# Placing the small products of a recurrent stage in TensorE's queue: one place and one bank for each kind, the turn of A ahead of the inverse, another last stage and opening

## The chip, the cores and the metric

The kernel runs on one core of a Trainium2 chip. The engines work side by side, each through its own queue in order: TensorE (PE, with its weight loads as PEld), VectorE (DVE), ScalarE (ACT), GpSimd (POOL) and SyncE (SP), which only issues transfers. The metric is the device time of one execution in microseconds (us). The kernel before took 3183.36 us, the median of three runs (3176.78, 3183.36 and 3184.9).

## The reference

One block of a streaming encoder, in float32: 2048 rows of width 1024.

```python
h = rms_norm(x, pre_mix_g);  proj = h @ w_in          # 1536 attention, 1792 RWKV, 2048 gate columns
y_a = chunk_band_attention(q, k, v, rel_bias)          # own chunk of 64 and 8 chunks before it
y_b = rwkv7_time_mix(p_rwkv, ...)                      # 8 heads of 64; delta rule over time:
#   state = state * w_t + (state @ a_t) b_t^T + v_t k_t^T;   y_t = state @ r_t
merged = sigmoid(gA) * (y_a @ proj_a) + sigmoid(gB) * (y_b @ proj_b)
x = x + rms_norm(merged @ w_out, post_mix_g)
x = x + rms_norm(relu(rms_norm(x, pre_ffn_g) @ w_up) ** 2 @ w_down, post_ffn_g)
```

## The kernel before

**Stages.** The 2048 rows are worked in four groups of 512 (g = 0 to 3). Each group goes through a recurrent stage (`phase_rwkv`), an attention stage and a merge; then two halves of 1024 rows each go through an up stage (`phase_up`) and a down stage (`phase_down`), which ends with the last norm and the output (`final`). The opening (`first_norm`) makes the first group's normed input.

**Dense products.** A projection of 128 columns (`dense`) is 24 TensorE matmuls of 128x512: weight and input are each split into a high and a low part, and three products of parts over 8 blocks of the inner dimension are summed in a bank of the pool `pd` (`psd` in the trace). A recurrent stage has 30 of them: 14 mixes (block 12 is the decay and rate input, 13 the gate input, p, 4 + p and 8 + p are r, k and v of head pair p) and 16 gates, so 720 dense matmuls. They are counted in the order of the program in the list `self.dl`; "place n" below means behind dense matmul n of the stage.

**Small products.** For each of the four head pairs p there are further: `lora` (tiles `ps_z`, `ps_a`), the sums of squares (`ps_ss`), the centred values (`ps_v`), the bonus (`ps_bonus`), the transposes of B and K (`ps_bk`), the chunk products (`ps_A`; 8 chunks in two halves, a matmul for each of the two heads, whose sums go to one bank a head), the turn of A (`ps_at`) and the products of values (`ps_w`). VectorE then inverts a 64x64 triangle for all chunks of two pairs at once (`rwkv_inverse`, 31 steps of two small operations each); `rwkv_blocks` joins the 32x32 blocks (`ps_t`), `rwkv_trans` makes the transition of each chunk (`ps_ug`, `ps_tq`, `ps_y`, `ps_s`), `recurrence` goes through the 8 chunks (for each chunk two matmuls into `ps_st` and two into `ps_y` for each head pair, then a VectorE step that makes the next state), and `rwkv_post` norms and gates the result (`ps_yt`, `ps_g`).

**Order.** A planner in the framework orders each engine's queue: it takes what is ready by its own model, the earlier in the program first. `queue_behind` ties an instruction behind another in the queue without a semaphore, and `place` does that with a place n among the stage's dense matmuls. Before, seven constants hold places: the blocks (`BLOCKS`), one turn (`TURNED`), one step of the recurrence (`FIFTH`), two parts of the bonus, the first chunk product (`SCORES`) and one pair's `ps_yt` (`TURNS`). `GATES` and `STEPS` say how many gates or steps of the recurrence are written between the parts of `rwkv_pre`. In the program, pairs 0 and 1 come first, then their inverse with gates, then the recurrence of pairs 0 and 1 woven into the preparation of pairs 2 and 3, then the second inverse and recurrence.

**Banks.** PSUM's 8 banks are two each for the pools `pd` (dense), `pa` (tag "a"), `pr` (tag "wus") and `py` (tag "y"). Nearly all small products go through the two banks of `pa`; the second half of the chunk products of pairs 0 and 1, the steps and `ps_yt` use `pr`; the outputs Y and `ps_g` use `py`.

**The end.** In the last step of `phase_down` each of four row tiles gets its last bank added (`gather`, L1469), and `final` squares it with a sum on ScalarE (L1480), multiplies by the gain on VectorE (L1481), adds two sums and takes the root on POOL (L1483, L143, L145), scales and adds x in two halves on VectorE (L1487) and stores (L1491).

Of the kernel before, what the change touches and what calls it, by code (L numbers as in the profile page):

```python
# [18 lines left out]
P = 128  # L19
D = 1024  # L20
# [14 lines left out]
STEPS = (1, 2, 1, 1, 1, 1, 1, 1, 1, 1, 1, 0, 0, 2, 1)  # L35
BLOCKS = ((412, 424), (640, 653))
TURNED = 438
FIFTH = 494
BONUS = {(0, 1): 138, (1, 0): 258}
SCORES = 150  # L40
TURNS = {1: (588, 592)}
# [15 lines left out]
class Block:  # L57
# [45 lines left out]

    def placed(self):

        for ins, n in self.places:
            self.queue_behind(ins, self.dl[n])
# [10 lines left out]
    def dense(self, col):  # L118
# [9 lines left out]
        if first:  # L128
# [5 lines left out]
            self.queue_behind(self.mm[0], self.last_transpose)  # L134
# [162 lines left out]
    def first_norm(self, sp, pt):  # L297
# [12 lines left out]
        squares = [self.root_of(sp, x, t) for t, x in enumerate(xs)]  # L310
# [113 lines left out]
    def lora(self, par, p):  # L424
        ps = self.pa.tile([P, G], F32, tag="a", name=("ps_z", "ps_a")[par])
        pc = slice(p * P, (p + 1) * P)
        self.nc.tensor.matmul(ps, self.wh[par][:, pc], self.lo[par], start=True, stop=False)
        self.nc.tensor.matmul(ps, self.wl[par][:, pc], self.lo[par], start=False, stop=True)
        return ps
# [14 lines left out]
    def rwkv_pre(self, g, p, rp, NA, between=lambda: None):  # L444
# [5 lines left out]
        self.mix(g, p, r)  # L450


        ps = self.lora(0, p)
        tw = self.tmp("tw")
        nc.scalar.activation(tw, ps, AF.Tanh, scale=0.5, bias=self.hw0[:, col])
        k = self.tmp("k")
        self.mix(g, 4 + p, k)

        ps = self.lora(1, p)
        ta = self.tmp("ta")  # L460
        nc.scalar.activation(ta, ps, AF.Tanh, scale=0.5, bias=self.ha0[:, col])
        v = self.tmp("v")
        self.mix(g, 8 + p, v)

# [7 lines left out]
        nc.scalar.activation(E[:, :, 1 : C + 1], cum3, AF.Exp)  # L472
# [11 lines left out]
        pss = self.pa.tile([P, GT, 2], F32, tag="a", name="ps_ss")  # L484
        for t in range(GT):
            nc.tensor.matmul(pss[:, t], sq[:, t * P : (t + 1) * P], self.bones2, start=True, stop=True)
# [33 lines left out]
        nc.vector.scalar_tensor_tensor(r, r, self.rk[:, col], tk, op0=ALU.mult, op1=ALU.mult)  # L520
        rh, rl = (self.tp.tile([P, G], F32R, tag="t", name="r" + x) for x in "hl")
        self.split(rh, rl, r)

        between()

        SV = rp.tile([P, NC, 2, C], F32, tag="SV", name="SV")
        psv = self.pa.tile([P, GT, P], F32, tag="a", name="ps_v")
        for t in range(GT):
            nc.tensor.matmul(psv[:, t], v[:, t * P : (t + 1) * P], self.cmat, start=True, stop=True)
        SVv = SV.rearrange("p (t h) e c -> p h t e c", h=2)  # L530
        for h in range(2):
            src = psv[h * C : h * C + C]
            nc.scalar.copy(SVv[C:P, h, :, 0], src[:, :, 0:C])
            self.values = nc.scalar.copy(SVv[0:C, h, :, 1], src[:, :, C:P]).ins
        R["SV"] = SV

        between()

        psb = self.pa.tile([P, G], F32, tag="a", name="ps_bonus")
        for i, x in enumerate((rh, rl)):  # L540
            mm = nc.tensor.matmul(psb, self.bones, x, start=i == 0, stop=i == 1)
            if (p, i) in BONUS:
                self.place(mm, BONUS[p, i])
# [4 lines left out]
        for h in range(2):  # L548
            cs = slice(h * 4, h * 4 + 4)
            pst = self.pa.tile([P, 4, 2, C], F32, tag="a", name="ps_bk")  # L550
            for j in range(4):
                nc.tensor.transpose(
                    pst[:, j].rearrange("p e f -> p (e f)"),
                    BK[:, h * 4 + j].rearrange("p s t -> p (s t)"), self.ident,
                )
            nc.vector.tensor_tensor(
                BR[:, cs, :, 0], pst, n2[:, cs, :, None].to_broadcast((P, 4, 2, C)), ALU.mult
            )

        between()  # L560
# [3 lines left out]
        for h in range(2):  # L564
            pool, tag = (self.pr, "wus") if p < 2 and h else (self.pa, "a")
            both = [pool.tile([P, 4, P], F32, tag=tag, name="ps_A") for _ in range(2)]
            for j in range(4):
                c = h * 4 + j
                for par, psA in enumerate(both):
# [5 lines left out]
                    if p == c == par == 0:  # L575
                        self.place(mm, SCORES)
            for par, psA in enumerate(both):
# [6 lines left out]
                for i in range(2):  # L584
                    hw = slice(par * C + 32 * i, par * C + 32 * i + 32)
                    cs = slice(h * 4, h * 4 + 4)
                    nc.scalar.copy(NA[hw, q, cs], BR[hw, cs, par, 2, 32 * i : 32 * i + 32])
        R["AR"], R["BR"] = AR, BR
        return R

    def rwkv_inverse(self, NA, rp):
# [23 lines left out]
        XD = ip.tile([P, 2, NC, 32], F32, tag="N", name="XD")  # L615
        nc.vector.transpose(XD, X1)
        XT = rp.tile([P, 2, NC, C], F32, tag="XT", bufs=1, name="XT")
        for par in range(2):
            r0 = par * C
            nc.gpsimd.memset(XT[r0 + 32 : r0 + 64, :, :, 0:32], 0.0)  # L620
            nc.scalar.copy(XT[r0 + 32 : r0 + 64, :, :, 32:64], XD[r0 + 32 : r0 + 64])
        for par in range(2):
            nc.gpsimd.tensor_copy(XT[par * C : par * C + 32, :, :, 0:32], XD[par * C : par * C + 32])
        self.X1, self.XT = X1, XT

    def rwkv_blocks(self, Rs, b):
# [3 lines left out]
        Z = self.ip.tile([P, 2, NC, 32], F32, tag="Z", name="Z")  # L630
# [16 lines left out]
        for mm, n in zip((first[0], second[0]), BLOCKS[b]):  # L647
            self.place(mm, n)
# [5 lines left out]
    def rwkv_trans(self, p, R):  # L654

        nc, xp = self.nc, self.xp
        AR, SV, XT, BR = (R[x] for x in ("AR", "SV", "XT", "BR"))
        rows = [slice(0, C), slice(C, P)]
        halves = [slice(0, 4), slice(4, 8)]

        WA = xp.tile([P, NC, 2, C], F32, tag="WA", bufs=1, name="WA")
        ps = self.pa.tile([P, 4, P], F32, tag="a", name="ps_at")
        for j in range(4):
            mm = nc.tensor.transpose(ps[:, j], AR[:, 1, 2 * j : 2 * j + 2].rearrange("p c t -> p (c t)"), self.ident)
            if p == j == 0:
                self.place(mm, TURNED)
# [3 lines left out]
        ps = self.pa.tile([P, NC, C], F32, tag="a", name="ps_w")  # L670
# [964 lines left out]
```

## Time and profile before

The profiled execution took 3181.86 us, of which its span, from the first to the last instruction, is 3180.2 us.

| stretch, us from the span's start | what | length, us | PE busy, us | DVE busy, us | ACT busy, us |
|---|---|---|---|---|---|
| 24 to 285 | recurrent stage, g = 0 | 261.0 | 258.70 | 184.99 | 130.92 |
| 478 to 748.6 | recurrent stage, g = 1 | 270.6 | 268.54 | 188.83 | 135.38 |
| 965 to 1236 | recurrent stage, g = 2 | 271.0 | 268.93 | 189.01 | 135.55 |
| 1453 to 1724 | recurrent stage, g = 3 | 271.0 | 268.93 | 189.25 | 135.68 |
| 1941 to 2246 | up stage, first half | 305.0 | 305.00 | 225.74 | 155.47 |
| 2555 to 2864 | up stage, second half | 309.0 | 306.65 | 230.99 | 155.92 |
| 2864 to 3169.2 | down stage, second half | 305.2 | 305.16 | 165.63 | 123.54 |
| 3169.2 to 3180.2 | after the last matmul | 11.0 | 0.00 | 6.14 | 1.34 |

A float32 matmul of the program (all small products but `ps_z`, `ps_a`, `ps_bonus` and `ps_g`) stands in the trace as two instructions: 64 chunk products of a stage are 128 rows of `ps_A`. A busy PE is not a PE at its peak: a matmul's busy time holds its latency, and neighbours overlap. Where the time of a matmul matters, the distance from one start to the next is to be read, from the starts in the timeline.

### The profile page before, as it was taken

To read this page: it belongs to the slowest core of one execution; us is meant where nothing else is said; L and a number is where in the kernel's file an instruction comes from. 1 tells how busy PE (TensorE), PEld (TensorE's weight loads), DVE (VectorE), ACT (ScalarE), POOL (GpSimd) and SP (SyncE) were. 2 spreads that over 40 slices of the span, in tenths; PEclk is the share of its full clock that TensorE was granted. 3 is DMA by queue.
4 is the path that set the end of the run, shared out by engine and by line. 5 is a ranking of instruction groups with operands and counts; after the bars stand their busy time and mean duration, and the time that the engine had idled before them with its cause. 6 is when DMAs were issued, how large, how long until landed. Compare 5 with 4: busy or idle time off the path is not lost.

```text
span 3180.2 us, 49723 instructions
## 1 busy us (share of the span) xinstructions
PE 3135.3 (99%) x18736; PEld 2567.8 (81%) x18736; DVE 2190.1 (69%) x3652; ACT 1617.5 (51%) x2639; POOL 570.8 (18%) x1087
## 2 busy tenths in 40 slices
PE   8999999999999999999999999999999999999998
PEld 6877788788888878888877888888888878888887
DVE  6776666777867676766776776877656668765564
ACT  5545645545745455745545745445543454444343
POOL 3121012122112122111122100221211122210000
PEclk9999999999999999999999999999999999999999
DMA  6245473257573256574246466554877766547664
GB/s 195 84 150 179 141 251 130 65 169 262 172 262 120 77 163 242 173 262 138 84 134 234 160 222 249 201 172 162 304 245 269 280 217 207 172 152 248 192 219 175
DMA packets 197477, 598.81 MB, mean 188 GB/s; under 512 B 25570, under 2 KB 25708, under 8 KB 197236
## 3 DMA queue, kind: packets, MB, share of 16 engines
q1 hardware_dynamic: 139124, 415.24, 40.0%
q0 software_dynamic: 48896, 163.61, 13.7%
q10 hardware_dynamic: 9216, 16.78, 1.4%
q8 instruction: 147, 2.41, 0.3%
q14 instruction: 94, 0.77, 0.1%
HBM read 431.67 MB, written 167.01 MB: 188 GB/s over the span
## 4 chain that ended last, share of the span: by engine, by line
PE 60%; issue 10%; POOL 2%; DMA 2%; ACT 2%; DVE 1%; SPq 0%; POOLq 0%; DVEq 0%; ACTq 0%
PE ps_dn L1454 19%; PE psd L92 16%; PE ps_u L92 9%; PE ps_o L1163 3%; PE ps_p L92 2%; PE ps_pv L1003 2%; POOL xd L1324 2%; PE ps_s L973 1%; PE ps_pt L992 1%; PE ps_A L571 1%; PE ps_tq L695 0%; DMA x<-in_x_dram 0%; PE ps_ht L1202 0%; PE ps_ug L684 0%; PE ps_st L723 0%
## 5 line engine op out<-in xcount | busy, mean ns | idle before, releaser
L1454 PE MATMUL ps_dn<-fop 128*128 128x512 f32 x2688 | 611.0, 389 | 0.5 <-DVE fop L83 0.5
L1454 PEld LDWEIGHTS ps_dn<-fop 128*128 128x128 f32 x2688 | 504.1, 188 | 105.4 <-DVE fop L83 0.9
L83 DVE TENSOR_TENSOR wlo<-wraw,whi 128x1024 fp32r<-128x1024 f32 x230 | 280.8, 1221 | 142.5 <-ACT whi L81 62.3
L81 ACT CAST whi<-wraw 128x1024 fp32r<-128x1024 f32 x232 | 243.4, 1049 | 232.5 <-PE psd L92 152.5
L92 PE MATMUL psd<-hh,whi 128*128 128x512 f32 x1328 | 355.7, 398 | 3.4 <-ACT k L400 3.4
L92 PE MATMUL psd<-hh,wlo 128*128 128x512 f32 x1328 | 358.1, 398 | 0.0
L92 PE MATMUL psd<-hl,whi 128*128 128x512 f32 x1328 | 356.3, 397 | 0.0
L92 PEld LDWEIGHTS psd<-hh,wlo 128*128 128x128 f32 x1328 | 243.6, 188 | 50.1
L92 PEld LDWEIGHTS psd<-hh,whi 128*128 128x128 f32 x1328 | 242.2, 188 | 51.7 <-ACT k L400 3.9
L92 PEld LDWEIGHTS psd<-hl,whi 128*128 128x128 f32 x1328 | 243.9, 188 | 47.3
L83 DVE TENSOR_TENSOR fop<-xraw,fop 128x1024 fp32r<-128x1024 f32 x112 | 137.0, 1223 | 175.3 <-ACT fop L81 174.9
L81 ACT CAST fop<-xraw 128x1024 fp32r<-128x1024 f32 x112 | 117.7, 1051 | 249.4 <-PE ps_dn L1454 189.6
L1324 POOL DMA_DIRECT2D xd<-X x192 | 103.7, 540 | 380.7 <-ACT X L1321 318.4
L83 DVE TENSOR_TENSOR fop<-wdraw,fop 128x1024 fp32r<-128x1024 f32 x112 | 136.6, 1220 | 19.0 <-ACT fop L81 18.8
L81 ACT CAST fop<-wdraw 128x1024 fp32r<-128x1024 f32 x112 | 117.7, 1051 | 36.7 <-DMA wdraw<-in_w_down_dram 21.7
L979 DVE CUSTOM_DVE_ANT_0 sc<-bias,ps_s 128x640 f32<-128x640 f32 (+4 forms) x128 | 93.8, 733 | 39.6 <-PE ps_s L973 23.5
L986 ACT ACTIVATE sc<-sc,mn 128x640 f32<-128x640 f32 (+4 forms) x128 | 97.8, 764 | 32.1 <-DVE mn L979 30.9
L997 DVE TENSOR_TENSOR PTl<-ps_pt,PTh 128x640 fp32r<-128x640 f32 (+4 forms) x128 | 94.4, 737 | 27.7 <-ACT PTh L996 26.8
L81 ACT CAST s12h<-s 128x1024 fp32r<-128x1024 f32 x32 | 33.7, 1053 | 155.2 <-PE ps_u L92 155.2
L92 PE MATMUL ps_p<-yh,whi 128*128 128x512 f32 x256 | 101.4, 399 | 2.7 <-ACT yh L81 1.7
L92 PE MATMUL ps_p<-yl,whi 128*128 128x512 f32 x256 | 101.2, 396 | 0.3 <-DVE yl L83 0.2
L1163 PE MATMUL ps_o<-whi,mh 128*128 128x512 f32 x256 | 100.4, 392 | 0.8 <-DVE o L1174 0.8
(370 smaller groups left out, 6731.8 us busy)
## 6 DMA issues: line engine op xcount, KB each, us to landing
wraw<-in_w_in_dram SPq DMA_DIRECT2D x168, 512.0 KB, 3.6
xraw<-xd SPq DMA_DIRECT2D x112, 512.0 KB, 4.3
xd<-X POOLq DMA_DIRECT2D x192, 256.0 KB, 4.6
wraw<-in_w_up_dram SPq DMA_DIRECT2D x80, 512.0 KB, 4.5
wdraw<-wd SPq DMA_DIRECT2D x64, 512.0 KB, 4.7
wdraw<-in_w_down_dram SPq DMA_DIRECT2D x48, 512.0 KB, 4.8
gd<-gate ACTq DMA_DIRECT2D x64, 256.0 KB, 2.2
wd<-cmb POOLq DMA_DIRECT2D x64, 256.0 KB, 4.0
```

Of the source, the lines that this page charges most:

```text
L81: high = self.high = self.nc.scalar.copy(hi, src)
L83: self.low = lower.tensor_tensor(lo, src, hi.bitcast(F32), ALU.subtract).ins
L92: mm.append(nc.tensor.matmul(ps, l, r, start=n == 0, stop=n == last).ins)
L571: mm = nc.tensor.matmul(psA[:, j].rearrange("p (s t) -> p s t", t=C), BK[rw, c].rearrange("p s t -> p (s t)"), AR[rw, :, c], start=True, s ...
L973: nc.tensor.matmul(pss[:, c0 + lo_ : c0 + lo_ + w], q[:, par, qs], Kv[:, k0 + lo_ : k0 + lo_ + w], start=i == 0, stop=i == 1,)
L979: least = nc.vector.tensor_tensor_reduce(sc[:, 0:n], bias[:, s0:640], pss[:, c0 : c0 + n], 1.0, 3.0e38, ALU.add, ALU.min, mn,)
L986: nc.scalar.activation(sc[:, 0:n], sc[:, 0:n], AF.Exp, scale=-1.0, bias=mn, accum_out=sm[:, col : col + 1])
L997: nc.vector.tensor_tensor(lv, pst[:, 0:nk], hv.bitcast(F32), ALU.subtract)
L1003: nc.tensor.matmul(pv[:, half], st, x[:, kt], start=i == 0, stop=i == len(terms) - 1)
L1163: nc.tensor.matmul(ps[t], l[:, k, ts], r[:, k % 2], start=k == 0 and j == 0, stop=k == KB - 1 and j == 2)
L1324: nc.gpsimd.dma_start(self.xd[q][i // 2][:, i % 2], src)
L1454: nc.tensor.matmul(ps, o[:, l, k, sl], o[:, r, k], start=start and n == 0, stop=stop and n == end)
```

## The change

1. The seven constants of places become one table `PINS`, with a place for the first matmul of each kind and pair, and `BANKS`, which gives some kinds a bank of `pr` ("r") or `py` ("y") in place of `pa` ("a").
2. The turn of A (`rwkv_turn`) and the products of values (`rwkv_values`) leave `rwkv_trans`; they are written ahead of the inverse or beside it. `rwkv_trans` then takes both pairs: first both `ps_ug`, then `ps_tq`, `ps_y` and `ps_s` of each. WA and GT get two buffers, S0 shares GT's.
3. The copies to NA are four a pair in place of eight. Z lies in XD's tile.
4. The order of the program: pairs 2 and 3 are prepared before the first recurrence is woven in (`STEPS`), pair 3's lora and values come later, `lora_g` (mix 13 and the load and split of g2) moves from the first inverse to behind the first recurrence, and the end of `rwkv_post` of pairs 2 and 3 is written ahead of the last gates.
5. The opening issues 38 matmuls of a constant (`bones`) around the four transposes, and 5 more between the first dense matmuls.
6. `final` of one tile is written behind the gather of the next; the root takes two POOL operations in place of three; in the second half the first columns' gain goes to a tile of its own, x has four buffers, and for the last four tiles the output is stored in two halves.

```diff
+STEPS = (0, 0, 0, 0, 0, 0, 0, 0, 0, 0, 0, 0, 0, 0, 5, 2)
+IDLE = (24, 0, 4, 4, 6)
+BETWEEN = 5
+LAST = 0
+PINS = {
+    "E3": 456, "na2": 462, "st05": 497, "g1": 602, "g3": 712, "g2": 702, "g0": 520,
+    "yt01": 520, "yt00": 520, "yt31": 712, "yt30": 712, "yt21": 700, "yt20": 700, "rh3": 472,
+    "x1": 626, "bk31": 474, "bk30": 474, "bo3": 474, "x0": 440,
+    "z0": 48, "a0": 48, "ss0": 110, "v0": 110, "bk00": 131, "bk01": 131, "bo0": 131, "at0": 131, "A00": 146, "A01": 146,
+    "z1": 146, "a1": 146, "ss1": 227, "v1": 227, "w0": 227, "bk10": 240, "bk11": 240, "bo1": 246, "at1": 240,
+    "A10": 258, "A11": 258, "z2": 290, "a2": 290, "w1": 290,
+    "ss2": 350, "v2": 350, "bk20": 384, "bk21": 384, "bo2": 390, "at2": 545, "A20": 396, "A21": 396,
+    "z3": 404, "a3": 404, "w2": 545, "t10": 440, "ss3": 456, "v3": 474, "t20": 456, "ug0": 470, "ug1": 470,
+    "at3": 600, "w3": 600, "yt10": 600, "yt11": 600, "t11": 626, "t21": 639, "ug2": 652, "ug3": 652,
+}
+BANKS = {
+    **{f"bk{p}{h}": "r" for p in range(2) for h in range(2)}, "A01": "r", "A11": "r",
+    "at0": "y", "z1": "y", "a1": "y", "w0": "y", "at1": "y", "w1": "y",
+    "bk20": "r", "bk21": "r", "at2": "a", "w2": "a", "A21": "r", "at3": "a", "w3": "a", "bo1": "y", "bo2": "y", "z3": "y", "a3": "y",
+}
...
+    def pin(self, mm, name):
+        if name in PINS:
+            self.place(mm, PINS[name])
+    def bank_of(self, name):
+        pool, tag = {"a": (self.pa, "a"), "r": (self.pr, "wus"), "y": (self.py, "y")}[BANKS.get(name, "a")]
+        return lambda shape, label: pool.tile(shape, F32, tag=tag, name=label)
...
-            self.queue_behind(self.mm[0], self.last_transpose)
+            self.queue_behind(self.mm[0], self.last_idle)
+            if self.idle is not None:
+                for i in range(BETWEEN):
+                    self.queue_behind(self.mm[i + 1], self.idle(1, self.mm[i]))
+                self.idle = None
...
+                mm = self.nc.tensor.matmul(
+                    idle, self.bones, self.bones[:, None, :].to_broadcast((P, 4, P)), start=True, stop=True
+                ).ins
...
+        turn(IDLE[0])
+        for t, x in enumerate(xs):
+            squares.append(self.root_of(sp, x, t))
+            self.queue_behind(self.last_transpose, last)
+            turn(IDLE[t + 1], self.last_transpose)
...
-            pool, tag = (self.pr, "wus") if p < 2 and h else (self.pa, "a")
-            both = [pool.tile([P, 4, P], F32, tag=tag, name="ps_A") for _ in range(2)]
+            bank = self.bank_of(f"A{p}{h}")
+            both = [bank([P, 4, P], "ps_A") for _ in range(2)]
...
+        for q, R in enumerate(Rs):
+            GT = R["GT"] = xp.tile([P, NC, C], F32, tag="GT", name="GT")
+            pool, tag = banks[q]
...
+            yield
+        for q, R in enumerate(Rs):
+            TQ = R["TQ"] = xp.tile([P, NC, 2, C], F32, tag="TQ", name="TQ")
...
-                    nc.scalar.activation(sq, u[t][:, ns], AF.Square, accum_out=ssq[:, n : n + 1])
-                    nc.vector.tensor_tensor(u[t][:, ns], u[t][:, ns], gt[:, ns], ALU.mult)
+                    nc.scalar.activation(sq, u[t][:, ns], AF.Square, scale=D ** -0.5, accum_out=ssq[:, n : n + 1])
+                    w = u[t][:, ns] if n or not half else op.tile([P, G], F32, tag="ug", name="ug")
+                    self.gained = nc.vector.tensor_tensor(w, u[t][:, ns], gt[:, ns], ALU.mult).ins
...
+                    if th == 0 and t + 1 < GT:
+                        self.queue_behind(scaled.ins, self.gained)
+                    if half and th == 0:
+                        nc.sync.dma_start(self.out[rows, ns], u[t][:, ns])
...
-                            advance(ends[t])
+                            advance(ends[t], 1)
+                            if t:
+                                advance(ends[t - 1])
```

More of the change, by code (lines that the diff above doesn't have):

```diff
@@ L309, in first_norm, with turn @@
         self.bank(pt)
-        squares = [self.root_of(sp, x, t) for t, x in enumerate(xs)]
+        idle = pt.tile([P, 4, P], F32, tag="tr", name="ps_idle")
+        last = None
+        def turn(n, behind=None):
+            nonlocal last
+            for i in range(n):
+                mm = self.nc.tensor.matmul(
+                    idle, self.bones, self.bones[:, None, :].to_broadcast((P, 4, P)), start=True, stop=True
+                ).ins
+                if behind is not None:
+                    self.queue_behind(mm, behind)
+                if last is not None:
+                    self.queue_behind(mm, last)
+                last = mm
+            return last
+        turn(IDLE[0])
+        squares = []
+        for t, x in enumerate(xs):
+            squares.append(self.root_of(sp, x, t))
+            self.queue_behind(self.last_transpose, last)
+            turn(IDLE[t + 1], self.last_transpose)
+        self.idle, self.last_idle = turn, last
         highs = self.scale_up(range(KB))
@@ L442, in lora_g, with rwkv_pre @@
         self.split(*self.lg, lg)
-    def rwkv_pre(self, g, p, rp, NA, between=lambda: None):
+    def rwkv_pre(self, g, p, rp, NA, out, between):
         nc = self.nc
@@ L646, in rwkv_blocks @@
                     second.append(mm)
-        for mm, n in zip((first[0], second[0]), BLOCKS[b]):
-            self.place(mm, n)
+        self.pin(first[0], f"t1{b}")
+        self.pin(second[0], f"t2{b}")
         for lo, hi in parts:
@@ L688, in rwkv_trans @@
-        yield
-        TQ = xp.tile([P, NC, 2, C], F32, tag="TQ", name="TQ")
-        for h, cs in enumerate(halves):
-            ps = self.pa.tile([P, 4, 2, C], F32, tag="a", name="ps_tq")
-            for j in range(4):
-                c = h * 4 + j
-                for par in range(2):
-                    nc.tensor.matmul(
-                        ps[rows[par], j], GT[rows[par], c], BR[rows[par], c, par, 0:2], start=True, stop=True
-                    )
-            nc.vector.tensor_tensor(
-                TQ[:, cs, 0], ps[:, :, 0], self.id64[:, None, :].to_broadcast((P, 4, C)), ALU.add
-            )
-            nc.vector.tensor_tensor(TQ[:, cs, 1], ps[:, :, 1], AR[:, 0, cs], ALU.add)
@@ L818, in rec_of @@
                 yield
-                for q in range(2):
-                    yield from self.rwkv_trans(2 * b + q, Rs[q])
-                    yield
+                yield from self.rwkv_trans(b, Rs)
                 yield from self.recurrence(b, Rs)
@@ L827, in phase_rwkv @@
             between = places(GATES, gate)
-            Rs = [self.rwkv_pre(g, q, rp, NA, between) for q in range(2)]
+            Rs, nxt = [], []
+            for q in range(2):
+                advance(self.rwkv_pre(g, q, rp, NA, Rs, between))
             advance(spread)
@@ L842, in phase_rwkv @@
             between = places(STEPS, lambda n: advance(rec, n))
-            nxt = [self.rwkv_pre(g, 2 + q, rp, NA, between) for q in range(2)]
-            inv = self.rwkv_inverse(NA, rp)
-            for n in (1, 4):
-                advance(rec, n)
-                gate()
+            second, third = (self.rwkv_pre(g, 2 + q, rp, NA, nxt, between) for q in range(2))
+            advance(second, 2)
+            advance(third, 1)
+            advance(second)
+            advance(third)
+            inv = self.rwkv_inverse(NA, rp, 1)
+            advance(rec, 1)
+            gate()
+            advance(rec, 4)
+            gate()
             advance(rec)
+            self.lora_g(g)
             post = [self.rwkv_post(q, Rs[q]) for q in range(2)]
@@ L851, in phase_rwkv @@
                 advance(p, 1)
+            for q in range(2):
+                nxt[q]["WA"] = self.rwkv_turn(2 + q, nxt[q]["AR"])
+                self.rwkv_values(2 + q, nxt[q])
             sums = []
```

251 lines of the change are left out of this document (149 added, 102 removed), and 21 rows, old and new, of the table PINS.

## The prediction

> **What bounds the kernel now.** I read the page first, then the busy times by stretch, then the starts of TensorE's instructions in the timeline.
>
> ```profile
> span 3180.2 us, 49723 instructions
> ...
> PE 3135.3 (99%) x18736; PEld 2567.8 (81%) x18736; DVE 2190.1 (69%) x3652; ACT 1617.5 (51%) x2639; POOL 570.8 (18%) x1087
> ...
> 478.00:748.60 270.60, 268.54 (x2230) 216.66 (x2229) 188.83 (x404) 135.38 (x245) 62.44 (x118) 1.00 0.42 142
> ...
> 3109.62 59.55 PE L1454 MATMUL ps_dn<-fop 128*128 128x512 f32 x262
> ```
>
> TensorE sets the end: it is busy for 99% of the span, the next engine for 69%. The third line is a recurrent stage by engines (PE, PEld, DVE, ACT, POOL): TensorE has no idle to speak of there either. So a gain must come from inside TensorE's busy time. The last line gives the measure: 262 dense matmuls in 59.55 us, 227 ns each. A recurrent stage has 720 of them, 163.4 us; the other 107 us of its 270.6 go to small products, to what lies around them, and to waits. What can be won is in those 107 us, four times.
>
> ```profile
> 719.50 0.28 PE L727 MATMUL ps_y<-ST,TQ 64*64 64x64 f32 x4
> 719.62 0.28 PE L723 MATMUL ps_st<-ST,TQ 64*64 64x64 f32 x4
> 719.74 0.28 PE L727 MATMUL ps_y<-ST,TQ 64*64 64x64 f32 x4
> 719.95 0.73 PE L92 MATMUL psd<-hh,whi 128*128 128x512 f32 x2
> 720.61 0.33 PE L723 MATMUL ps_st<-ST,TQ 64*64 64x64 f32 x4
> ```
>
> Read by starts: two dense matmuls between two small groups take 0.66 us in place of 0.45, and the last group of four ahead of them 0.21 in place of 0.12. A visit to 64x64 products thus costs some 0.30 us beside its work.
>
> **The change part by part, a recurrent stage first.** *Chunk products.* These are the dearest small products.
>
> ```profile
> 515.20 1.16 PE L571 MATMUL ps_A<-AR,BK 64*128 64x128 f32 x16
> 516.29 1.88 PE L92 MATMUL psd<-hh,whi 128*128 128x512 f32 x7
> ...
> 541.97 1.16 PE L571 MATMUL ps_A<-AR,BK 64*128 64x128 f32 x8
> 543.06 0.73 PE L92 MATMUL psd<-hh,wlo 128*128 128x512 f32 x2
> ...
> 551.71 1.78 PE L571 MATMUL ps_A<-AR,BK 64*128 64x128 f32 x16
> 553.41 0.73 PE L92 MATMUL psd<-hh,wlo 128*128 128x512 f32 x2
> ...
> 621.23 2.02 PE L571 MATMUL ps_A<-AR,BK 64*128 64x128 f32 x16
> 623.18 0.96 PE L92 MATMUL psd<-hh,wlo 128*128 128x512 f32 x3
> ```
>
> Sixteen rows that alternate between the two heads take 1.09 us, and eight rows of one head alone also take 1.09 us: the two heads run beside each other only where both have a bank. Pair 0, whose first half has a place already, needs 2.18 us in all. Pair 1 goes in pieces (8 rows, 8 rows, 16 at 1.70): 3.88 us. Pair 2 goes as 16 rows at 1.95 and twice 8: 4.13 us. Pair 3 goes in four eights: 4.36 us. With A10, A11 at 258 and A20, A21 at 396, each with one half on "a" and one on "r" and the banks' last users 12 to 46 dense matmuls earlier, four banks are free and I count 2.18 us for each: 1.70 and 1.95 us saved. Pair 3 keeps both halves on "a" and I count nothing (2.18 us at best). Pairs 1 and 2 also make one visit each instead of three, 4 x 0.30 us; but the products of values get visits of their own at 227, 290, 545 and 600, in place of three beside the recurrence. Net between 0 and 1.2 us; I take 0.6.
>
> *The recurrence's own products.* Before, they are mixed with the preparation of the later pairs:
>
> ```profile
> 612.90 0.33 PE L712 MATMUL ps_y<-SV,BR 128*64 128x64 f32 x2
> 613.27 1.16 PE L529 MATMUL ps_v<-cmat,v 128*128 128x128 f32 x8
> 614.36 1.09 PE L695 MATMUL ps_tq<-BR,GT 64*64 64x128 f32 x16
> 615.38 0.45 PE L712 MATMUL ps_y<-SV,BR 128*64 128x64 f32 x8
> ...
> 619.28 0.50 PE L92 MATMUL psd<-hh,wlo 128*128 128x512 f32 x1
> ...
> 713.99 1.03 PE L712 MATMUL ps_y<-SV,BR 128*64 128x64 f32 x27
> ```
>
> From 612.90 to 619.28 stand 32 `ps_y` rows (some 1.0 us in one piece, by the last line), 32 of `ps_tq` (twice 1.02), 8 of `ps_v` (0.9), a bonus and a group of `ps_bk` (0.45 each): 4.8 us of work in 6.38, because the shape changes nine times. With both `ps_ug` at 470 and 652 and the rest in order behind them, the shapes follow each other in blocks. The second recurrence has little of this mixing now, and in the first one v3, bk3 and bo3 at 474 still come beside it. I take 2.2 us a stage, between 0 (it stays mixed) and 4 (two and a half stretches like this one).
>
> *Waits.* The turn and the products of values leave the chain ahead of `ps_ug`, and the preparation's ScalarE work leaves the first steps of the recurrence:
>
> ```profile
> 630.60 1.66 PE L92 MATMUL psd<-hh,whi 128*128 128x512 f32 x6 [0.85 <-ACT k L400]
> ...
> 708.61 1.96 PE L684 MATMUL ps_ug<-WA,XT 64*64 64x128 f32 x32 [0.45 <-ACT WA L675]
> ```
>
> Both should go: 1.3 us. What is late next is what has a place and isn't ready there. A place holds TensorE's whole queue, so the dense matmuls behind it wait too, and ScalarE and VectorE behind those. The tightest that I find are ss0 and v0 at 110, where pair 0's v ends at 96, and `ps_yt` of pairs 2 and 3 at 700 and 712, behind a recurrence that I expect to end near 676. The second inverse isn't among them: its first chunk products now come some 148 dense matmuls ahead of place 626. From both sides: nothing, or several waits like the 0.85 us one; I take one, 0.85 us. Fewer NA copies and POOL and SP issues that move (mix 13's weights, g2's load, yd's store) lie beside a busy TensorE with idle SP and POOL; nothing, and 0.3 us a visit if a weight comes late. `lora_g`, moved behind the first recurrence, ends with mix 13 at 480, 40 dense matmuls (9 us) ahead of g0 at 520; nothing. S0 in GT's buffer waits for that pair's `ps_tq`, which stands ahead of it in TensorE's queue anyway; nothing.
>
> A stage: 1.70 + 1.95 + 0.6 + 2.2 + 1.3 - 0.85 = 6.9 us; four stages 27.6 us.
>
> *Opening.*
>
> ```profile
> 17.12 4.70 PE L131 MATMUL psd<-hh,whi 128*128 128x512 f32 x11 [0.15 <-ACT whi L81]
> ...
> 18.63 1.28 ACT L378 CAST hh<-xt 128x512 fp32r<-128x512 f32 x2 [0.53 <-DVE xt L375]
> ...
> 21.66 2.00 PE L131 MATMUL psd<-hh,wlo 128*128 128x512 f32 x8
> ```
>
> From 17.12 to 21.66 a matmul takes 413 ns, and 227 afterwards: the clock was not granted in full yet. If the 38 early matmuls wake it, the last two of these run when hh is cast, at 19.91, and end 0.5 us later: 1.2 us, less 0.2 for a0, which now stands at 48 beside z0: 1.0 us. At worst the idle matmuls count for nothing and the five between are in the way: a loss of 5 x 0.227 = 1.1 us. At best 1.3.
>
> *Last stage.*
>
> ```profile
> 3161.04 0.69 DVE L1469 TENSOR_TENSOR u<-u,ps_dn 128x512 f32<-128x512 f32 x1 [10.11 <-PE ps_dn L1454]
> 3161.77 0.63 ACT L1480 ACTIVATE squ<-u 128x512 f32<-128x512 f32 x1 [12.28 <-DVE u L1469]
> ...
> 3162.57 0.70 POOL L1483 TENSOR_TENSOR ssqu<-ssqu 128x1 f32<-128x1 f32 x1 [72.65 <-ACT squ L1480]
> ...
> 3163.63 0.55 POOL L145 TENSOR_TENSOR rs_r<-rs_v,nhalf 128x1 f32<-128x1 f32 x1
> ...
> 3165.54 0.68 DVE L1469 TENSOR_TENSOR u<-u,ps_dn 128x512 f32<-128x512 f32 x1
> ...
> 3170.03 1.28 DVE L1469 TENSOR_TENSOR u<-u,ps_dn 128x512 f32<-128x512 f32 x2
> ...
> 3175.18 1.41 DVE L1487 SCALAR_TENSOR_TENSOR u<-u,rs_r,x1r 128x512 f32<-128x512 f32 x2
> ```
>
> A bank is full every 12 x 0.227 = 2.72 us, but a gather comes every 4.5 us, since in VectorE's queue it stands behind the scaling of the tile before, which waits for ScalarE and POOL. The last matmul ends at 3169.2, VectorE at 3176.6. Written one tile apart, VectorE has 0.69 + 0.69 + 1.42 = 2.8 us a tile and keeps up: last gather at 3169.2, its gain done at 3170.5, tile 2 scaled at 3171.9; the root of tile 3 comes at 3169.9 + 0.73 + 0.70 + 0.55 and two handovers of 0.07, 3172.0; all scaled at 3173.5. I take 3.0 us (2.0 if POOL's one wide operation is slower than its two, 3.5 if the half stores land sooner).
>
> *Up stage, second half.* The same order at the end of the first down stage ends VectorE's gains sooner.
>
> ```profile
> 2577.04 0.50 PE L92 MATMUL ps_u<-bh,a1h 128*128 128x512 f32 x1 [2.35 <-DVE x L1319]
> ...
> 2577.90:2581.20 3.30, 3.30 (x9) 2.58 (x8) 1.44 (x2) 2.77 (x4) 0.54 (x1) 0.50 1.03 416
> ```
>
> This wait of 2.35 us, and 3.3 us at half the clock behind it (the 0.50), come from VectorE's queue there. By the sum above its finals end 0.7 us sooner; I take 0.7 us, of 0 to 4.0.
>
> **Sum:** 27.6 + 1.0 + 3.0 + 0.7 = 32.3 us off the profiled execution's 3181.86 us (1.7 us more than its span): 3149.6. The median of the runs shown lies 1.5 us above that execution, so 3151.
>
> **The rivals.** *The halves don't pair.* The places only say "not before"; if the planner still finds one bank free, A stays in eights. Pair 0 speaks against: with a place it pairs. Then 1.70, 1.95 and 0.6 drop out: 4 x 2.65 + 4.7 = 15.3 us, 3168.
>
> *All of it.* No new waits, pair 3 paired, mixing gone, the 2.35 us wait and its slow clock gone: up to 59.7 us, 3124; I give this case what lies below 3137.
>
> *Waits eat the stages' gain.* Inputs are as late as before and only the holder changes. TensorE's idle is 1% already, which speaks for it: 4.7 us remain, 3179.
>
> *Slower: bank "a" in the first recurrence.* Behind 470, fourteen tiles go through its two banks: ug0, tq0 and S0's two each, v3, bk30, bk31, bo3 and A3's four.
>
> ```profile
> L580 DVE SCALAR_TENSOR_TENSOR BR<-ps_A,n,masks 128x128 f32<-128x128 f32 x64 | 17.6, 343 | 5.2 <-PE ps_A L571 5.2
> ...
> L698 DVE TENSOR_TENSOR TQ<-ps_tq,id 128x256 f32<-128x256 f32 x8 | 3.4, 425 | 20.5 <-PE ps_tq L695 20.5
> ```
>
> Each is emptied by two operations of 0.42 us or four of 0.34. If places force them in a row, each waits some 0.84 us for the one two before it: 14 x 0.84 x 4 = 47 us against gains of 35.7 (with no other new wait): 11.3 us slower, 3195. It decides from 0.64 us a tile. Against it: bank "a" carries more tiles there now, and dense matmuls fill in.
>
> *One long wait a stage, with the clock.* A wait like the 2.35 us one in each stage, with half of 3.3 us lost behind it, costs 4 x 4.0 = 16 us: 3167. The Trainium skill (TensorE: Matmul & The Clock Gate, "HAM oscillation") puts the drop to half clock at idle gaps beyond about 3.4 us; by it such a wait would cost no clock and the case would end at 3160. This trace disagrees: the row above stands at 0.50 behind a wait of 2.35 us, so the row decides.
>
> **How the numbers follow.** My forecast (3137 to 3163) 0.53; all of it 0.12; halves don't pair 0.10; long waits with the clock 0.05; waits eat the gain 0.12; slower 0.08. A measurement of this kernel tells 0.3%, 9.5 us, from no change: below 3173.8 lie the first four, 0.80; within it 0.12; above it 0.08. The range leaves out the lowest part of "all of it" and the slower case: 3130 to 3179.
>
> **What would show it.** Right: `ps_A` in groups of 32 rows with about 2.2 us between starts for pairs 0 to 2; no 0.85 us wait behind the recurrence's first steps; a stage near 264 us; matmuls at 227 ns from the first dense one; VectorE's last operation about 4.4 us behind the last matmul. Wrong: waits of TensorE at places 110, 131, 474, 520, 700 or 712 that add to more than 1 us a stage, or `ps_A` still in eights.

## The result, and the profile after

The changed kernel takes 3128.4 us, the median of six runs (3124.76 to 3131.25), beside 3179.65 us for the kernel before in the same job (3176.78 to 3184.9): a ratio of 0.9836, 95% interval 0.9823 to 0.9849. Its profiled execution took 3128.76 us.

The page's first lines after, with the busy time of each engine, and below them the recurrent stage of g = 1 from the view by stretches (length; busy us and rows of PE, PEld, DVE, ACT, POOL; granted clock; DMA share; GB/s):

```profile
span 3127.1 us, 49685 instructions
...
PE 3101.5 (99%) x18779; PEld 2558.5 (82%) x18779; DVE 2174.7 (70%) x3652; ACT 1605.4 (51%) x2575; POOL 580.3 (19%) x1071
...
464.20:720.50 256.30, 255.76 (x2220) 211.15 (x2220) 183.77 (x402) 131.10 (x227) 65.06 (x120) 1.00 0.43 142
```

TensorE is as full as it was; it has 34 us less to do and stands idle 19 us less. The stage is 14.3 us shorter than the 270.60 us of before. By the starts, this stretch holds 759 dense matmuls and that one 768, so 2.0 us lie in the count and 12.2 us in the small products and the waits. Attention gives some of it back: from the first dense matmul of a stage to the first matmul into `ps_o` in the merge, the four groups are 13.6, 10.8, 11.3 and 12.7 us shorter, 48.4 in all. The rest of the 53.1 us between the two spans: second up stage 3.2, behind the last matmul 2.4, ahead of the first dense 0.3, less 0.8 and 0.4 us more in the first down and up stage.

What became shorter in the stage is seen in the same view with one line of code at a time (length; busy PE, PEld and, in the first row, DVE). Before, in this order: chunk products, `ps_y` from values, `ps_tq`, `ps_ug`, `ps_y` of the steps:

```profile
478.00:748.60 270.60, 15.36 (x128) 13.07 (x128) 17.63 (x64) 1.00 0.42 142
478.00:748.60 270.60, 7.37 (x128) 5.61 (x128) 1.00 0.42 142
478.00:748.60 270.60, 8.56 (x128) 6.79 (x128) 1.00 0.42 142
478.00:748.60 270.60, 7.86 (x128) 6.92 (x128) 1.00 0.42 142
478.00:748.60 270.60, 9.03 (x128) 6.70 (x128) 1.00 0.42 142
```

After, the same five:

```profile
464.20:720.50 256.30, 10.19 (x128) 9.04 (x128) 17.08 (x64) 1.00 0.43 142
464.20:720.50 256.30, 4.61 (x128) 4.06 (x128) 1.00 0.43 142
464.20:720.50 256.30, 7.75 (x128) 7.00 (x128) 1.00 0.43 142
464.20:720.50 256.30, 7.42 (x128) 6.94 (x128) 1.00 0.43 142
464.20:720.50 256.30, 8.45 (x128) 6.41 (x128) 1.00 0.43 142
```

Each kind has its 128 rows in both. The chunk products lose 5.2 us of busy time, the four kinds of the recurrence 2.8 + 0.8 + 0.4 + 0.6 = 4.6 us. Read by starts (each row from its start to the next row's), which leaves no overlap, the same parts are 4.8 and 4.9 us, the stretch between dense matmuls beyond 227 ns each 1.4 us (9.4 to 8.0), and `ps_g`, `ps_ss`, `ps_v` and the rest 1.1 us net: 12.2 us, the whole stage.

TensorE's rows in the timeline after (start, length, and idle with what ended it), chunk products of pair 0 (those of pairs 1 and 2 are alike at 536.00 and 575.01), the block ahead of the first recurrence, pair 3, and the longest wait of the stage:

```profile
502.28 2.06 PE L662 MATMUL ps_A<-AR,BK 64*128 64x128 f32 x32
504.26 0.50 PE L123 MATMUL psd<-hh,whi 128*128 128x512 f32 x1
...
599.05 3.71 PE L793 MATMUL ps_ug<-WA,XT 64*64 64x128 f32 x64
602.60 1.91 PE L809 MATMUL ps_tq<-BR,GT 64*64 64x128 f32 x32
604.44 1.15 PE L819 MATMUL ps_y<-SV,BR 128*64 128x64 f32 x32
605.42 1.10 PE L824 MATMUL ps_s<-SV,BR 128*64 128x64 f32 x32
606.46 1.96 PE L809 MATMUL ps_tq<-BR,GT 64*64 64x128 f32 x32
608.35 1.15 PE L819 MATMUL ps_y<-SV,BR 128*64 128x64 f32 x32
609.33 1.10 PE L824 MATMUL ps_s<-SV,BR 128*64 128x64 f32 x32
610.37 0.33 PE L836 MATMUL ps_st<-st,TQ 64*64 64x64 f32 x4
...
615.69 1.71 PE L662 MATMUL ps_A<-AR,BK 64*128 64x128 f32 x16
...
618.84 1.16 PE L662 MATMUL ps_A<-AR,BK 64*128 64x128 f32 x8
...
620.34 1.16 PE L662 MATMUL ps_A<-AR,BK 64*128 64x128 f32 x8
...
708.51 1.04 PE L868 MATMUL ps_yt<-ident,yn 128*64 128x128 f32 x8 [0.35 <-DVE yn L859]
```

A pair's 32 rows go in one piece of 1.98 us (502.28 to 504.26). The recurrence's products of both pairs stand in one block of 11.32 us (599.05 to 610.37) without a dense matmul or a foreign shape in it. Pair 3 still goes as 16, 8 and 8.

### The profile page after: what moved, and what is told of

Read it like the earlier page. It is cut to its first block, busy times and chain, and to the rows that moved or that the text cites. A ratio compares the mean times of both kernels' runs of the same rounds, so it can differ in the third digit from the quotient of the medians.

```text
span 3127.1 us, 49685 instructions
## 1 busy us (share of the span) xinstructions
PE 3101.5 (99%) x18779; PEld 2558.5 (82%) x18779; DVE 2174.7 (70%) x3652; ACT 1605.4 (51%) x2575; POOL 580.3 (19%) x1071
## 5 line engine op out<-in xcount | busy, mean ns | idle before, releaser
L123 PE MATMUL psd<-hh,whi 128*128 128x512 f32 x1328 | 362.4, 399 | 0.1
L123 PE MATMUL psd<-hl,whi 128*128 128x512 f32 x1328 | 349.8, 396 | 0.0
L1120 ACT CAST PTh<-ps_pt 128x640 fp32r<-128x640 f32 (+4 forms) x128 | 79.9, 624 | 41.5 <-PE ps_pt L1116 40.5
```

The costliest lines, as they stand in the source:

```text
L123: mm.append(nc.tensor.matmul(ps, l, r, start=n == 0, stop=n == last).ins)
L1120: nc.scalar.copy(hv, pst[:, 0:nk])
```

## The experiments

Times are medians, ratios those to the kernel before on the same chip. The changed kernel itself was timed in its own job alone, so small differences from it are read from the traces. Where a stage's length is given, it is that of g = 1 from the start of its first dense matmul to 227 ns behind the start of its 720th, 255.9 us before and 247.4 after; in the other stages the differences are alike unless said. (These two lengths are only 8.5 us apart because before the change the last small products stood behind the 720th.)

**One bank for both halves.**

```diff
-    ... "A01": "r", "A11": "r",
-    ... "A21": "r",
```

> The changed kernel with the second halves of the chunk products of pairs 0, 1 and 2 back on bank "a"; all places stay. Theory P (the pairing of the heads is worth what it saves on TensorE): the second half of each of these pairs goes in two pieces of 1.09 us in place of one of 1.0, some 1.2 us more a pair, and each pair makes two visits more at about 0.3 us: 3 x (1.2 + 0.6) = 5.4 us a stage, 21 us in all, so 3150 us. Rival V (only the number of visits counts, the pieces are hidden): 3 x 0.6 x 4 = 7 us, 3136. Rival N (the pairing is worth nothing, the places alone brought the gain): within 3 us of 3128.

3166.75 us, 0.9959 (0.9944 to 0.9974): 38 us lost, more than any theory had. The stage is 254.5 us, 7.1 more. By starts: chunk products 3.8 us and some 1 us for four visits, which is theory P; and one wait. TensorE's row:

```profile
595.72 1.13 PE L662 MATMUL ps_A<-AR,BK 64*128 64x128 f32 x8 [2.11 <-DVE BR L671]
```

Pair 2's second half needs the bank that VectorE has yet to empty, and VectorE is in the last steps and the 1.13 us transpose of the first inverse. In the stages of g = 0 and 2, 11.7 and 10.2 us longer, half a clock follows it (last section).

So a bank of its own is worth its pairing, 3.8 us a stage, about 1 us of visits, and 2.1 us more because it lets TensorE run ahead of an engine that is late.

**Pair by pair.** The loop over both pairs is called for one pair, then for the other:

```diff
...
-                yield from self.rwkv_trans(b, Rs)
+                for q in range(2):
+                    yield from self.rwkv_trans(b, Rs, (q,))
```

> The changed kernel with ug, tq, y and S0 of one pair ahead of those of the other, as before the change, in place of both ug first; places and banks stay, and the products still stand in a row with no dense matmul between them. Theory W (both ug first hides the emptying of a bank behind the other pair's products): ps_tq waits for ScalarE's copy of the first ug, 0.5 to 1 us for each pair, 8 pairs in four stages twice over: 8 to 16 us more, 3136 to 3145. Rival M (all that counts is that each kind stands in one run): within 3 us of 3128.

3140.55 us, 0.9880 (0.9863 to 0.9896): 12 us lost, the size that theory W had, but on another path. The stage is 250.3 us. TensorE's rows of the first recurrence, to be held against the block above:

```profile
601.59 1.96 PE L793 MATMUL ps_ug<-WA,XT 64*64 64x128 f32 x32
603.48 0.33 PE L819 MATMUL ps_y<-SV,BR 128*64 128x64 f32 x2
603.80 2.13 PE L809 MATMUL ps_tq<-BR,GT 64*64 64x128 f32 x32
605.86 1.09 PE L819 MATMUL ps_y<-SV,BR 128*64 128x64 f32 x29
```

No wait is shown, and yet 0.65 us a pair are gone: while ScalarE copies GT, the planner puts two rows of `ps_y` in between. By starts these two take 0.32 us, `ps_tq` behind them takes 0.2 us more than in the block above and `ps_ug` 0.1 more, so the changes of shape cost, not a wait. The block lasts 12.62 us (601.59 to the first step at 614.21) in place of 11.32. The second recurrence shows the same pattern and lasts 12.89 us in place of 11.31, so the two are the stage's whole 2.9 us.

**Pair 3 paired.**

```diff
+    "A30": 477,
+    "A31": 486,
```

> The changed kernel with two places more: the halves of pair 3's chunk products at 477 and 486, so that both banks "a" are empty for each half and both heads run beside each other. Theory P (pairing): 16 and 16 rows in about 1.0 us each in place of 1.64, 1.08 and 1.08, so 1.8 us less, and a visit less, 0.3 us: 2.1 us a stage, 8 us in all, 3120. Rival W (a wait takes its place: VectorE, which empties the banks, is behind at 486, or the second inverse comes late at 626): 3128 or above.

3121.86 us, 0.9818 (0.9803 to 0.9832): 6.5 us below the changed kernel by the medians, though the intervals of the two ratios overlap; by the traces the four stages carry 5.1 of it. The stage is 246.2 us, 1.2 less where 2.1 were expected. Rows of `ps_A` there:

```profile
615.61 1.16 PE L664 MATMUL ps_A<-AR,BK 64*128 64x128 f32 x16
...
619.58 1.16 PE L664 MATMUL ps_A<-AR,BK 64*128 64x128 f32 x16
```

Both heads run beside each other; by starts 1.6 us are saved and 0.4 given back around the steps.

**The turn late.**

A's turn and the products of values of pairs 0 and 1 are issued behind the inverse again, without their places and banks.

```diff
...
-        if p < 2:
-            R["WA"] = self.rwkv_turn(p, AR)
...
                 self.rwkv_blocks(Rs, b)
                 yield
+                if b == 0:
+                    for q in range(2):
+                        Rs[q]["WA"] = self.rwkv_turn(q, Rs[q]["AR"])
+                        self.rwkv_values(q, Rs[q])
```

> The changed kernel with A's turn and the products of values of pairs 0 and 1 back between the inverse and ug, on bank "a" and without places. Theory W (they stood in the chain ahead of ug): waits of ScalarE's WA ahead of ug of 0.5 to 1 us, twice at most, and the visits move without one being saved: 1 to 1.5 us a stage, 4 to 6 us, 3133. Rival N (the chain ahead of ug has room since ug's place, 470, sets it): within 1.5 us of 3128.

3132.28 us, 0.9856 (0.9841 to 0.9871); the stage is 247.6 us, 0.2 more (1.0 in g = 0). The time fits theory W's 3133, but its mechanism isn't there: no wait stands ahead of `ps_ug`. The profiled execution is 3.6 us longer than the changed kernel's, and its two largest differences lie outside the recurrent stages: 2.0 us from the first `ps_p` of g = 0 to the next stage, where half a clock stands for 3.4 us, and 2.0 in the second up stage. So rival N: under the place of `ug` the turn's earlier place is worth nothing that the stages show.

**Places taken away.** First all of them (`PINS = {}`), then those of the preparation of pairs 0 to 2, then those of the inverses, of `ug`, of one step and of the turn and values of pairs 2 and 3.

> The changed kernel with an empty list of places; banks, turn and order of issue stay. Theory P (the places carry the gain): half of the chunk products unpaired, 1 to 2 us, the products of values of pair 1 in nine pieces of one to three, 9 x 0.2 to 0.3 us, and waits as in the kernel whose steps alone were put in blocks (5.8 us a stage between dense matmuls): 5 to 10 us a stage, 3148 to 3168. Rival B (banks and order of issue carry it, the places only tidy up): 2 us a stage at most, 3136.

> The changed kernel without the places of the preparation of pairs 0 to 2 (z, a, ss, v, bk, bo, at, A and the products of values of pairs 0 and 1); the places of the inverse, of ug, of pair 3 and of the last products stay, and all banks. Without any places a stage took 17 us more. Theory A (the preparation's places carry most of that, by chunk products and values in one piece each): chunk products +2.5 us, values in nine pieces +1.6, some eight visits more at 0.2 to 0.3 us and bk, bonus and v between them +1.4: 7 to 8 us a stage, 3158. Rival W (the waits behind the inverse and the last products carry it, and those places stay): under 4 us a stage, below 3144.

> The changed kernel without the places of the inverse (t1, t2 and the copies x), of ug, of the fifth step and of the turn and values of pairs 2 and 3; the preparation's places and those of the last products stay. Theory A: the inverse waits where the planner puts it (2.8 us in the kernel without places) and ug and tq mix in the second recurrence (1.5 us): 4 to 5 us a stage, 3146. Rival W: both waits and the clock behind them, 8 us or more a stage, 3160 or above. Rival N (issue order alone keeps these in one run): under 1 us a stage, 3132.

Without any: 3194.62 us, 1.0051 (1.0036 to 1.0066), slower than the kernel before; the stage is 264.4 us, 17.0 more than with them, where theory P had 5 to 10. Without those of the preparation: 3162.16 us, 0.9952 (0.9937 to 0.9966), 256.1 us: chunk products 3.4 us, products of values in nine pieces 1.6, between dense matmuls 2.3, the rest 1.3; no long wait. Without the others: 3160.68 us, 0.9947 (0.9930 to 0.9964), 254.8 to 259.2 us, and here a wait leads, at the second inverse; TensorE's row and the stretch behind it, the clock at 0.61:

```profile
668.59 1.31 PE L704 MATMUL ps_t<-X,BR 32*32 32x32 f32 x64 [3.01 <-DVE X L680]
```

```profile
668.80:672.00 3.20, 3.20 (x68) 2.75 (x61) 1.65 (x3) 2.39 (x4) 2.55 (x4) 0.61 0.34 134
```

Without a place `ps_t` stands in the queue where X is not ready: VectorE is 3 us later, and the dense matmuls behind it, which are ready, stand too. The two groups of places are worth 8.6 and 7.3 to 11.7 us, together about the 17: theory A of the preparation, rival W of the recurrence.

**One part alone, in the kernel before.** Chunk products of pair 1 at 266; steps in blocks; then both again with the places behind them moved.

```diff
+                    if p == 1 and j == par == 0:
+                        self.place(mm, 266)
```

```diff
-STEPS = (1, 2, 1, 1, 1, 1, 1, 1, 1, 1, 1, 0, 0, 2, 1)
+STEPS = (1, 0, 0, 0, 0, 0, 0, 0, 0, 0, 0, 0, 5, 4, 0)
```

> The kernel before with one place more: the chunk products of pair 1 not ahead of dense matmul 266, so that both halves find four empty banks. Theory P (the forecast's term): 3.88 us in four pieces become 2.0 in one, 1.9 us, and three visits become one, 0.4: 2.3 us a stage, 9 us in all, 3170. Rival W (what comes behind has to wait, because the inverse gets its block 1 us later and its own places at 412 and 424 stay): back to 0 to 3 us in all, 3177 or above.

3192.18 us, 1.0044 (1.0028 to 1.0061): slower. By starts the chunk products do save 1.9 us a stage, theory P to the tenth. But the stage is 258.9 us, 3.0 more, for a place of before that stayed:

```profile
595.87 1.20 PE L639 MATMUL ps_t<-X,BR 32*32 32x32 f32 x64 [3.33 <-DVE X L616]
```

The first inverse needs pair 1's chunk products; they come later, and its place at 412 holds the whole queue. Behind the wait the clock stands at 0.50 for 3.4 us, from 597.70 to 601.10. The wait and the slow clock together cost 4.9 us, some 3.4 and 1.5, against the 1.9 saved.

> The kernel before with pair 1's chunk products at 266, as before, and with what follows moved by 16 dense matmuls (3.6 us, the wait that the place alone brought): the inverse's blocks at 428 and 440, the turn at 454, the fifth step at 510. Theory J (a place pays only when the places behind it move along): the 1.9 us of the chunk products and 0.2 us a visit stay won, 8 us in all, about 3170. Rival W (the wait only moves: the recurrence, late by 3.6 us, now meets the preparation of pair 3, and the second inverse waits): 3180 or above.

With `BLOCKS` at 428 and 440, the turn at 454 and the step at 510: 3205.83 us, 1.0078 (1.0061 to 1.0095), slower still, rival W. TensorE's and ScalarE's rows:

```profile
598.10 1.20 PE L639 MATMUL ps_t<-X,BR 32*32 32x32 f32 x64 [0.65 <-DVE X L616]
...
602.08 1.38 PE L92 MATMUL psd<-hh,whi 128*128 128x512 f32 x3 [1.87 <-ACT r L400]
```

```profile
599.55 1.25 ACT L623 COPY XT<-XD 32x512 f32<-32x512 f32 x2 [6.18 <-DVE XD L618]
...
601.34 0.68 ACT L400 ACTIVATE r<-psd,omu 128x512 f32<-128x512 f32 x1
```

The 3.33 us wait is down to 0.65, but a dense matmul now waits 1.87 us for a bank: ScalarE's queue stood 6.18 us at the inverse's copy, with the emptying of that bank (L400) behind it. Four more waits of 0.78 to 1.17 us follow in this stage, where the kernel before has one of 0.85, and half a clock for 3.4 us; the stage is 6.0 us longer than before.

> The kernel before with one line changed: the list that says how many steps of the first recurrence are issued at each point of the preparation of pairs 2 and 3, so that ug, tq, y and S0 of pairs 0 and 1 come behind pair 2's preparation, each kind in one run. No place, no bank and no turn is changed, and chunk products go in pieces as before. Theory M (mixing was the large term: ps_y, ps_tq, ps_ug and the dense matmuls between them cost 4 to 5 us a stage less after the change): 3 to 4 us a stage, 12 to 16 us in all, about 3165. Rival S (mixing is worth the 2.2 us a stage that the forecast gave it): 9 us, 3171. Rival N (order alone does nothing without places and banks): within 5 us of 3180.

> The kernel before with the steps of the first recurrence put in blocks, as in the run of that name, and the places of the second inverse moved from 640 and 653 to 652 and 665, since waits of 2.0 and 1.4 us stood there. Theory J: the waits go and what the blocks saved stays (ps_y 2.1 us, ps_bk, ps_ss and ps_z 0.7, chunk products 0.9, less 0.6 for three visits more): 2.5 to 3 us a stage, about 3168. Rival W (ScalarE's queue stands behind the second inverse wherever its place is): 3180 or above.

Steps in blocks: 3192.81 us, 1.0041 (1.0026 to 1.0056): slower, which none of the three theories had. By starts `ps_y` is 2.1 us shorter, chunk products 0.9, `ps_bk`, `ps_ss`, `ps_v`, `ps_z` and `ps_a` 1.0; between dense matmuls stand 5.8 us more, 1.8 and 1.1 of them waits around the second inverse. With that inverse's places 12 matmuls later: 3182.56 us, 1.0010 (1.0000 to 1.0019), so what the blocks save is just lost again. Of the 4.0 us more between dense matmuls, 1.8 lie in a wait like the last one. ScalarE's and TensorE's rows:

```profile
683.70 1.25 ACT L621 COPY XT<-XD 32x512 f32<-32x512 f32 x2 [4.80 <-DVE XD L616]
...
687.65 0.68 ACT L775 ACTIVATE gate<-psd,hgb 128x512 f32<-128x512 f32 x1
```

```profile
688.39 1.89 PE L92 MATMUL psd<-hh,whi 128*128 128x512 f32 x7 [1.64 <-ACT gate L775]
```

The changed kernel has places for just these copies on ScalarE (`x0` at 440, `x1` at 626), and for other work of that engine (`na2`, `E3`, `rh3`), so they are not queued ahead of what the dense matmuls need. That this is why it escapes the wait is argued from these rows alone. The copies' places were not taken away by themselves, and the run without the recurrence's places, which lacks `x0` and `x1` too, has its wait at VectorE's X.

**Finals, opening, last products.** Old finals in the changed kernel; the changed kernel without the early matmuls (`IDLE` and `BETWEEN` at 0); the paired kernel with `yt20`, `yt21` at 703, `g2` at 704, `yt30`, `yt31` at 715, `g3` at 716.

> The changed kernel with the end of the down stages as before: gain and scaling of a tile in a row, sums of squares scaled in POOL's second operation, one store a tile. Theory T (the new order of the finals is worth the difference behind the last matmul alone): 10.99 - 8.61 = 2.4 us more, 3131, and the second up stage stays near 306 us. Rival U (the 3.2 us that the second up stage lost come from that order too, as the forecast had it with 0.7): another 3.2 us in that stage, 3134, with a wait of over 2 us and half a clock in its first 10 us.

> The changed kernel without the 38 early matmuls and the five between the first dense ones. Theory C (they only bring the full clock forward): the first 11 dense matmuls take 413 ns each again up to about 21.5 us, and the third dense starts 1.4 us later: 1.4 us, 3130. Rival Z (they are in the way of the first dense ones as much as they help): within 0.5 us of 3128.

> The kernel with pair 3's chunk products paired (3121.9), and the last products (yt and g of pairs 2 and 3) two to four dense matmuls later, at 703, 704, 715 and 716, where VectorE's yn is ready. Theory W: the wait of 0.5 us ahead of ps_yt goes, and one visit with it: 0.5 to 1 us a stage, 3119. Rival N (the wait only moves on into attention, whose first products need the same engines): 3122.

Old finals: 3128.73 us, 0.9844 (0.9827 to 0.9860). From the last matmul to the end it takes 10.98 us in place of 8.61, theory T; the second up stage stays at 305.5 us, so rival U falls. The medians, 0.3 us apart, can't tell 2.4 us from nothing; the traces can.

No early matmuls: 3130.75 us, 0.9852 (0.9837 to 0.9866); the first stage is 252.4 us in place of 250.9, theory C. TensorE's rows there:

```profile
16.85 5.06 PE L172 MATMUL psd<-hh,whi 128*128 128x512 f32 x11 [0.15 <-ACT whi L112]
21.71 2.14 PE L172 MATMUL psd<-hh,wlo 128*128 128x512 f32 x8
```

Eleven in 4.86 us, 442 ns each; before the change it was 413. The first change of the clock that the trace lists stands at 21.99 us in this run, at 21.27 in the kernel before and at 5.41 in the changed kernel, where the early matmuls go from 427 to 230 ns there. So the early matmuls do bring the full clock forward.

Later last products: 3120.94 us, 0.9824 (0.9809 to 0.9838). The stage is 245.6 us, 0.6 less, and the wait at `ps_yt` is gone; the medians don't tell it from the paired kernel.

## Where the prediction was right, and where it failed

The direction and the likeliest mechanism were right: pairs 0 to 2 in groups of 32, no 0.85 us wait behind the first steps, the opening's dense matmuls at 0.23 to 0.34 us where they took 0.43 to 0.66, VectorE's end 5.0 us behind the last matmul where 4.4 were expected. The size was wrong: a stage takes 256.3 us where 264 were expected. The time, 3128.4, lies 1.6 us below the range and 22.6 below the forecast; of these, 19.8 lie in the four groups (48.4 measured, 27.6 and the opening's 1.0 forecast). By the forecast's own split a time below 3137 belongs to "all of it" (0.12), whose lowest part the range left out at 3130. Its conditions came in part only: the mixing went, but pair 3 was not paired, new waits of 0.8 us a stage came, and the 2.35 us wait was absent for another reason (below).

**The step that failed is the recurrent stage's mixing term, "I take 2.2 us a stage, between 0 (it stays mixed) and 4".** It measured 4.9 us by starts (4.6 by busy time), above its own upper end. The forecast priced one stretch, 612.90 to 619.28, and said of the second recurrence that it "has little of this mixing now". The rows of the kernel before had it there as well, for each pair: `ps_ug`, two rows of `ps_y`, `ps_tq`, the rest.

```profile
699.42 1.96 PE L684 MATMUL ps_ug<-WA,XT 64*64 64x128 f32 x32
701.32 0.33 PE L712 MATMUL ps_y<-SV,BR 128*64 128x64 f32 x2
701.64 2.13 PE L695 MATMUL ps_tq<-BR,GT 64*64 64x128 f32 x32
```

The pair-by-pair run puts that pattern back and loses 1.3 us in the first recurrence and 1.6 in the second. Another part is the `ps_y` of the steps, 1.4 us less, which the forecast didn't price; in the run of steps in blocks the order alone brings 1.3 of it. With `ps_g`, `ps_v` and others, 1.1 us more that the forecast had nowhere, the stage gives 3.8 us more than the term.

**Chunk products:** 3.65 us forecast, 4.8 by starts. Pairs 1 and 2 give 1.9 and 2.1, since 32 rows in one piece take 1.99 us and not twice 1.09; pair 0 gains 0.2 by it too, and pair 3, counted at nothing, 0.5 (3.81 in place of 4.34).

**Visits and waits:** 0.6 + 1.3 - 0.85 = 1.05 forecast, 1.4 measured between dense matmuls (57 stretches of them became 49). The new waits were sized well: 0.31 us at `ps_t` and 0.52 at `ps_yt`, by starts beyond 227 ns, 0.83 in all.

**Sum of a stage:** 6.9 forecast, 12.2 measured, of which attention gives back up to 1.4.

**Opening:** 1.0 forecast, 1.5 by the run without it; against the kernel before, the first stage gains 1.1 us more than the others. **Last stage:** 3.0 forecast, 2.4 measured. The working left POOL's one wide operation open at 2.0, and in this execution it is slow:

```profile
3120.09 1.22 POOL L1610 TENSOR_SCALAR rs_v<-ssqu 128x1 f32<-128x1 f32 x1 [0.85 <-ACT squ L1605]
...
3121.99 0.75 DVE L1615 SCALAR_TENSOR_TENSOR u<-u,rs_r,x1r 128x512 f32<-128x512 f32 x1 [0.76 <-POOL rs_r L1612]
```

The same instruction takes 0.64 us in the traces of six of the runs with these finals, and there the end comes 7.9 to 8.3 us behind the last matmul, in place of 8.6 here and 11.0 before. So the change is worth 2.4 to 3.1 us, and the forecast lay within.

**Second up stage:** 0.7 forecast as an effect of the finals, 3.2 seen, and the reason was wrong. With old finals in the changed kernel it is 305.5 us. In four kernels whose up and down stages are those of before it is 306.0 to 306.9, not 309.15. The run with the late turn, whose up stage is the changed one, has 307.95. So the 2.35 us wait of the profiled execution, and the clock behind it, most likely belong to that execution, not to the kernel, and some 3 of the 53.1 us between the two traces are not the change's; each kernel was traced only once.

**The rivals.** The waits that the slower ones feared are real: they came in the four runs that put one part into the kernel before, all slower than it but the last, which is the same. What keeps them out is the table of places as a whole: without it the stage is 17.0 us longer, and with it no idle time of TensorE in the stage above is over 0.35 us. Whether the table would do it alone, without the new banks, turn and order, was not run. The bank rival didn't come: behind place 470 TensorE is never idle for 0.1 us or more ahead of a product in bank "a".

## What to carry to other kernels

A place in an in-order queue holds everything behind it, so places are worth something as a schedule and cost something one by one: the same place for one kind of product that saves 1.9 us lost 3 where its consumer's place stayed. Price shape changes by counting them on the whole stage (starts, one kind at a time), not from one stretch. And read a stall that stands in one profiled execution against a second kernel with the same stage before it goes into a sum.

## What the runs showed of the hardware

In the one-bank run the same wait stands in all four stages: 2.05, 2.11, 2.06 and 2.03 us. Behind the first and the third the granted clock is at half for 10.2 and 6.8 us, behind the others it is full. These two stretches, with the clock in the last column but two:

```profile
137.79:148.03 10.24, 10.24 (x31) 7.98 (x31) 6.19 (x15) 1.37 (x2) 2.85 (x3) 0.50 0.11 25
1079.87:1086.70 6.83, 6.83 (x20) 5.18 (x20) 4.72 (x12) 1.37 (x2) 1.68 (x1) 0.50 0.00 0
```

So the length alone does not decide, and some 2 us can be enough. The Trainium skill (TensorE: Matmul & The Clock Gate, "HAM oscillation") names gaps beyond about 3.4 us; these rows disagree.

Where the wait falls is what differs. In each of the 16 traces, the changes of the clock stand whole multiples of 3.41 us apart, as on a grid. These are the steps of the grid in which the four waits lie, with TensorE's busy time behind the length:

```profile
134.38:137.79 3.41, 1.36 (x7) 0.83 (x7) 3.34 (x10) 1.56 (x3) 0.99 (x2) 1.00 0.06 25
591.77:595.18 3.41, 1.85 (x9) 1.16 (x7) 3.22 (x10) 2.22 (x3) 0.29 (x1) 1.00 0.25 99
1076.46:1079.87 3.41, 1.35 (x11) 1.00 (x9) 3.21 (x10) 1.18 (x2) 1.40 (x3) 1.00 0.00 0
1561.15:1564.56 3.41, 1.55 (x7) 0.94 (x5) 3.27 (x11) 1.97 (x3) 0.60 (x1) 1.00 0.17 66
```

In the first and the third the whole wait lies in one step, which is idle for 2.05 and 2.06 us; in the others the end of the step cuts the wait, and 1.56 and 1.86 us are left. Over the 16 traces, all 17 steps at full clock that were idle for 1.87 us or more were followed by half a clock. So were 14 of the 14629 that were idle for less, among them 10 of the 61 between 1.0 and 1.87 us; what sets those 14 apart stays open.

At the opening of the kernel without early matmuls the view's clock column reads 1.00 while eleven matmuls take 442 ns each:

```profile
18.00:20.00 2.00, 2.00 (x6) 1.52 (x5) 2.00 (x4) 1.62 (x4) 1.90 (x3) 1.00 0.94 302
```

The trace lists nothing of the clock ahead of 21.99 us, and where nothing is listed the view shows 1.00. There the distance between starts is to be read, not the clock.

The POOL operation on 128x1 that took 1.22 us (row above) stands 1.64 us behind the last matmul in ten traces with the same finals. It took 0.64 us in six of them and 1.22 in four, with VectorE at work throughout in all ten; what makes the difference stays open.
